# Some products and one copy move from VectorE to GpSimd, and the convolution history from GpSimd to ScalarE, in a streaming encoder layer

## The chip, the cores and the metric

The kernel runs on one core of a Trainium2 chip. A core has five engines with a queue of their own each, and each runs its queue in order: TensorE (PE, matrix products into PSUM; its weight loads are shown as PEld), VectorE (DVE), ScalarE (ACT), GpSimd (POOL) and SyncE (SP), which here only issues transfers (DMAs). An instruction that waits for a semaphore holds everything behind it in its queue. The metric is the time of one execution on the device in microseconds (us). The kernel before takes 2788.09 us, the median of three runs from 2786.51 to 2789.14.

## The reference, cut to what matters

One layer is applied to 1024 new positions (prompt) and 64 positions of a running stream (sample), together 1088 columns:

```
h    = RMSNorm(x) * (1 + scale1) + shift1
proj = h @ W_in                      # q, k, v, x, B, C, two gates, small columns, merge gates
q,k,v,x,B,C = silu(causal conv of width 4)   # the last 3 rows before the conv are an output, too
# mixer A, 8 heads, chunk by chunk (state s of 128 x 128):
lhs = I + strictly lower (k k^T * decay * beta)      # solved against v and k
u   = inv(lhs) (beta v) - inv(lhs) (beta exp(gam) k) s
o   = exp(gam) q s + (q k^T * decay) u
s   = exp(last) s + (k exp(last - gam))^T u
o   = rms(o) * gdn_norm * silu(z)
# mixer B, 8 groups of 4 heads, chunk by chunk (4 states of 128 x 64):
y   = (C B^T * decay * dt) x + exp(gam) C s ;   s = exp(last) s + B^T (wj x)
# then the merge of A and B, W_out, a norm, W_up, conv of width 3, silu gate, W_down, a norm
```

Here gam is the running sum of the log decays within a chunk and last its last value. The kernel's chunks are 128 positions: eight of the prompt and one of the sample.

## The kernel before

Channels lie on the 128 partitions and positions along the free dimension. A projection is done by tiles of 128 output channels; one tile takes three segments of 364, 364 and 360 columns, each of 24 matmuls into one of three PSUM buffers `pj` (8 slices of the model dimension, three matmuls each, because both factors are split in a rounded part and its rest: `whi`, `wlo` for weights). `load_w` brings a tile's weights (two DMAs into `wraw`), ScalarE makes `whi` by a cast (L114) and VectorE `wlo` by a subtraction (L115), one tile ahead of its use.

The first half of the kernel (the mixers, to about 1480 us) lays the chains of the mixers into the projections. Each chain is a generator; `weave` keeps a clock of PE work in `now` and takes the next piece of a chain when the latency named in the table `LAT` has gone by, else another 24 matmuls of a projection. The order of PE is written by hand that way, and fixed. The order on the other engines comes from the scheduler of the tile framework, which knows the dependences and its own estimates.

Three chains matter here, for head h of mixer A and group g of mixer B:

- `gdn_inverse`. `masked_decay` brings the decays `NU`: a DMA, a causal select on POOL (L587) and nine exponentials on ACT (L590). PE makes k k^T by chunks and DVE multiplies it in (L613). The diagonal is taken out by a product with the identity and a reduction (L618, L619), a reciprocal root of it follows in a dozen small DVE instructions on tile `kn` (L535 to L541), and `NU` is scaled (L626). Four DMAs (`dU`, L632) and three (`Ub`, L636) re-lay it, and the 32 x 32 blocks are inverted by 31 pairs of a DVE product and a reduction (L644, L647: the X loop). The result `Xb` is transposed in a copy (L649, XT below) and sent to memory and back by DMAs and transposed by DVE (L660). PE's products with it come `LAT["solve"]`, 74 us on `weave`'s clock, after the last k k^T.
- `gdn_scan`. The decays of q: a DMA, a select on POOL into `E` (L587), nine exponentials (L590), one more on ACT (L699), and two products with q (L700, L701). Then nine chunks in a row, of which each goes PE, DVE `r` (L740), PE, ACT `u` (L746), PE, DVE `st` (L756). At the end `o_norm` squares q and o on ACT (L777), adds the squares (L778), takes a reciprocal root of the column sums through a DMA, and scales `v` by it and by `gnorm` (L781).
- `ssd_mix`. For chunk c: a DMA of the decays into `gi`, a select on POOL (L821), four exponentials on ACT (L824), a fifth of `gi` (L826), and the decayed C (L827, half of C times the exponential, for four heads). `inputs` makes the matrices of the chunk one chunk ahead. In the chunk, the state is scaled (L874) and the new part added (L876).

`conv_steps` copies a projection's PSUM into `buf` by ACT and, at the last segment, copies the last three columns of prompt and sample into `ncm` by POOL (L517, L518).

Of the kernel before, what the change touches and what calls it, by code (L numbers as in the profile page):

```python
# [5 lines left out]

# [10 lines left out]
ALU = mybir.AluOpType  # L17
# [30 lines left out]
def body(tc, I, O):  # L48
# [28 lines left out]
    b_eps4 = bias_tile(4 * EPS, "beps4")  # L77

# [242 lines left out]
    with ExitStack() as c1:  # L321
# [183 lines left out]
        def conv_steps(w, ti, d):  # L505
            buf = tl(cv, [P, 1096], "buf", bufs=2)
            pool.memset(buf[:, 0:3], 0.0)
            pool.memset(d[:, CW:TW], 0.0)
            pool.tensor_copy(buf[:, 1027:1030], hist[:, ti, :])

            def evac(si, s, e, ps):
                if si < 2:
                    act.copy(buf[:, 3 + s:3 + e], ps[:, :e - s])
                else:
                    act.copy(buf[:, 3 + s:3 + TP], ps[:, :TP - s])
                    act.copy(buf[:, 1030:1094], ps[:, TP - s:T - s])
                    pool.tensor_copy(ncm[:, ti, 0:3], buf[:, 1024:1027])  # L517
                    pool.tensor_copy(ncm[:, ti, 3:6], buf[:, 1091:1094])  # L518
                    e = CW
                u = d[:, s:e]  # L520
                act.activation(u, buf[:, s:e], AF.Identity, bias=bcv[:, ti:ti + 1], scale=wcv[:, ti, 0:1])
                for i in range(1, 4):
                    dve.scalar_tensor_tensor(out=u, in0=buf[:, s + i:e + i], scalar=wcv[:, ti, i:i + 1], in1=u,
                                             op0=ALU.mult, op1=ALU.add)
                act.activation(buf[:, s:e], u, AF.Tanh, scale=0.5)
                dve.scalar_tensor_tensor(out=u, in0=buf[:, s:e], scalar=1.0, in1=u, op0=ALU.add, op1=ALU.mult)
            yield from project_steps(w, hx, evac)
# [70 lines left out]
        def gdn_inverse(h):  # L598
# [8 lines left out]
            for c0 in range(0, NC, 4):  # L607
                n = min(4, NC - c0)
                ps = tl(pp, [P, 4, P], "n")
                for c in range(c0, c0 + n):  # L610
# [7 lines left out]
            dve.tensor_tensor(out=dg, in0=NU[:, 0:8, :], in1=ident.unsqueeze(1).to_broadcast([P, 8, P]), op=ALU.mult)  # L618
# [7 lines left out]
            dve.scalar_tensor_tensor(out=NU, in0=NU, scalar=-1.0, in1=H.br.unsqueeze(2).to_broadcast([P, NC, P]),  # L626
                                     op0=ALU.mult, op1=ALU.mult)
# [21 lines left out]
            dve.tensor_copy(XT, X.rearrange("p j c -> p c j"))  # L649
# [41 lines left out]
        def gdn_scan(h):  # L691
# [8 lines left out]
            dve.tensor_tensor(out=gi[:, 0:8, :], in0=gi[:, 0:8, :], in1=chunks(q[:, 0:TP]), op=ALU.mult)  # L700
            dve.tensor_tensor(out=gi[:, 8, :], in0=gi[:, 8, :], in1=chunk(q, 8), op=ALU.mult)  # L701
# [70 lines left out]
        def o_norm(h):  # L772
# [5 lines left out]
            dve.tensor_tensor(out=sq[:, 0:CW + 1], in0=sq[:, 0:CW + 1], in1=q[:, 0:CW + 1], op=ALU.add)  # L778
            yield LAT["on"]
            yield from rsqrt_row(sq, (128 * EPS) ** 2 * 4)  # L780
            dve.scalar_tensor_tensor(out=v[:, 0:CW], in0=v[:, 0:CW], scalar=gnorm, in1=sq[:, 0:CW],  # L781
                                     op0=ALU.mult, op1=ALU.mult)
# [28 lines left out]
        def ssd_mix(g):  # L811
# [5 lines left out]
            def decay(c):  # L817
# [7 lines left out]
                if c > 0:  # L825
                    act.activation(gi, gi, AF.Exp, scale=-1.0)  # L826
                    dve.scalar_tensor_tensor(out=gi, in0=chunk(cm, c).unsqueeze(1).to_broadcast([P, 4, P]),  # L827
                                             scalar=0.5, in1=gi, op0=ALU.mult, op1=ALU.mult)
# [25 lines left out]
            for c in range(NC):  # L854
# [18 lines left out]
                if s is not None:  # L873
                    dve.tensor_tensor(out=sn, in0=s, in1=ebl[:, c, h4].unsqueeze(2).to_broadcast([P, 4, 64]),  # L874
                                      op=ALU.mult)
                    dve.tensor_tensor(out=sn, in0=pst, in1=sn, op=ALU.add)  # L876
                else:
                    dve.tensor_copy(sn, pst)
# [457 lines left out]
```

## Time and profile before

| | us |
|---|---|
| median of three runs | 2788.09 |
| the profiled execution | 2791.15 |
| its span in the trace | 2789.4 |
| PE busy in the span | 2726.9 (98%) |
| DVE busy | 1815.0 (65%) |
| ACT busy | 1257.5 (45%) |
| POOL busy | 185.5 (7%) |

The span runs from the first instruction to the end of the last; 1.8 us of the profiled execution lie around it. Busy time is the time in which an engine has an instruction in work. "Idle before" is the time in which it had none, and the releaser is what ended it. A chain of waits runs back from the last instruction through what released each.

### The profile page before, as it was taken

The numbers are of one execution on the slowest core, as the hardware profiler recorded it, in microseconds if no ns is written. First come the engines' busy times: TensorE is split into PE (matmuls) and PEld (weight loads), VectorE is DVE, ScalarE is ACT, GpSimd is POOL, SyncE is SP. The second block draws the span as 40 slices with busy tenths as digits, with TensorE's granted clock in tenths as the row PEclk, the third lists the DMA queues.
The fourth block names the chain that finished last, engine by engine and source line by source line (L and its number), as shares of the span: only waits on it lengthen the run. The fifth ranks groups of instructions, "written<-read, shape, count | busy, mean of one in ns | idle before, by whom it ended". The sixth has DMA issues, their size and how long they took to land.

```text
span 2789.4 us, 48767 instructions
## 1 busy us (share of the span) xinstructions
PE 2726.9 (98%) x18650; PEld 2638.5 (95%) x18650; DVE 1815.0 (65%) x3912; ACT 1257.5 (45%) x2888; POOL 185.5 (7%) x565
## 2 busy tenths in 40 slices
PE   6999999999999999999999999999999999999998
PEld 5999999999999999999999998999899999999998
DVE  5776579697887878777544557543766464555556
ACT  5644455465555545555443434212534242424244
POOL 0110001010010101101000000000000000000000
PEclk8999999999999999999999999999999999999999
DMA  6222323223241323323235765343211111111122
GB/s 228 96 67 89 112 66 110 79 81 110 71 115 61 112 75 95 98 81 100 69 100 200 257 199 172 123 142 92 85 50 46 46 43 41 46 45 47 39 61 73
DMA packets 212716, 266.72 MB, mean 96 GB/s; under 512 B 51995, under 2 KB 145019, under 8 KB 212483
## 3 DMA queue, kind: packets, MB, share of 16 engines
q1 hardware_dynamic: 212482, 263.62, 30.2%
q8 instruction: 146, 2.39, 0.4%
q14 instruction: 88, 0.71, 0.1%
HBM read 217.38 MB, written 46.13 MB: 94 GB/s over the span
## 4 chain that ended last, share of the span: by engine, by line
PE 88%; DVE 5%; DMA 4%; ACT 1%; issue 1%; SPq 0%; POOL 0%; DVEq 0%; ACTq 0%; POOLq 0%
PE pj L226 36%; PE pj L147 16%; PE sy L147 6%; PE gk L147 5%; PE gs L147 5%; PE sa L147 5%; PE sy L226 3%; PE gk L226 2%; DMA wada<-in_wada 2%; PE n L226 2%; PE gs L226 1%; DVE prod L644 1%; DMA gi<-gdr 1%; PE pj L1221 1%; DVE Xb L647 1%
## 5 line engine op out<-in xcount | busy, mean ns | idle before, releaser
L226 PE MATMUL pj<-h,whi 128*128 128x364 f32 x4560 | 1151.4, 334 | 1.6 <-DVE fz L897 1.6
L226 PEld LDWEIGHTS pj<-h,whi 128*128 128x128 f32 x4560 | 791.9, 188 | 8.6 <-issue 4.8
L226 PE MATMUL pj<-h,wlo 128*128 128x364 f32 x2280 | 747.5, 328 | 0.0
L147 PE MATMUL pj<-op,whi 128*128 128x364 f32 (+1 forms) x1904 | 476.6, 330 | 0.8 <-ACT op L188 0.6
L226 PEld LDWEIGHTS pj<-h,wlo 128*128 128x128 f32 x2280 | 428.7, 188 | 0.0
L114 ACT CAST whi<-wraw 128x512 fp32r<-128x512 f32 (+1 forms) x382 | 231.1, 617 | 370.3 <-PE pj L147 130.7
L147 PEld LDWEIGHTS pj<-op,whi 128*128 128x128 f32 x1904 | 337.2, 188 | 6.7 <-ACT op L188 1.6
L115 DVE TENSOR_TENSOR wlo<-wraw,whi 128x512 fp32r<-128x512 f32 (+1 forms) x382 | 258.0, 684 | 111.8 <-ACT whi L114 111.2
L147 PE MATMUL pj<-op,wlo 128*128 128x364 f32 (+1 forms) x952 | 312.5, 329 | 0.0
L1128 DVE SCALAR_TENSOR_TENSOR acc<-buf,wfc,acc 128x364 f32<-128x364 f32 (+1 forms) x264 | 156.6, 597 | 97.3 <-ACT acc L1126 93.2
L147 PEld LDWEIGHTS pj<-op,wlo 128*128 128x128 f32 x952 | 178.8, 188 | 0.0
L147 PE MATMUL sy<-op,whi 128*128 128x364 f32 (+1 forms) x672 | 167.8, 330 | 0.0
L147 PE MATMUL gs<-op,whi 128*128 128x364 f32 (+1 forms) x652 | 164.0, 331 | 1.2 <-ACT q L1005 1.0
L147 PE MATMUL sa<-op,whi 128*128 128x364 f32 (+1 forms) x644 | 161.4, 330 | 0.0
L147 PE MATMUL gk<-op,whi 128*128 128x364 f32 (+1 forms) x640 | 160.3, 331 | 0.0
L824 ACT ACTIVATE E<-E,dt 128x128 f32<-128x128 f32 x288 | 94.6, 396 | 80.1 <-POOL E L821 80.0
L147 PEld LDWEIGHTS sy<-op,whi 128*128 128x128 f32 x672 | 119.0, 188 | 1.0 <-issue 0.4
L147 PEld LDWEIGHTS gs<-op,whi 128*128 128x128 f32 x652 | 115.5, 188 | 3.5 <-ACT q L1005 1.3
L147 PEld LDWEIGHTS sa<-op,whi 128*128 128x128 f32 x644 | 114.0, 188 | 1.2 <-issue 0.6
L147 PEld LDWEIGHTS gk<-op,whi 128*128 128x128 f32 x640 | 113.7, 189 | 1.4 <-issue 0.6
L147 PE MATMUL sy<-op,wlo 128*128 128x364 f32 (+1 forms) x336 | 110.3, 328 | 0.0
L147 PE MATMUL gs<-op,wlo 128*128 128x364 f32 (+1 forms) x326 | 107.7, 330 | 0.0
(414 smaller groups left out, 4364.7 us busy)
## 6 DMA issues: line engine op xcount, KB each, us to landing
wraw<-in_win SPq DMA_DIRECT2D x158, 256.0 KB
wraw<-in_wup SPq DMA_DIRECT2D x88, 256.0 KB
gi<-gdr SPq DMA_DIRECT2D x72, 256.0 KB
wada<-in_wada SPq DMA_DIRECT2D x32, 512.0 KB
op<-spz SPq DMA_DIRECT2D x24, 544.0 KB
wraw<-in_wdown SPq DMA_DIRECT2D x40, 256.0 KB
spz<-fz SPq DMA_DIRECT2D x48, 182.0 KB
gt<-spg SPq DMA_DIRECT2D x48, 182.0 KB
```

Source lines behind the costliest of these rows:

```text
L114: act.copy(hi, src)
L115: dve.tensor_tensor(out=lo, in0=src, in1=hi, op=ALU.subtract)
L147: pe.matmul(pss[si][:, :e - s], lhsT=a[:, k, :], rhs=xk[:, b, s:e], start=(k == 0 and n == 0), stop=(k == nk - 1 and n == 2))
L226: pe.matmul(out, lhsT=lhsT, rhs=rhs, start=start, stop=stop)
L644: dve.tensor_tensor(out=prv, in0=X[:, 0:i + 1, 0:n].rearrange("p j c -> p c j"), in1=U[:, 0:i + 1, i:i + 1].rearrange("p j o -> p o j").to ...
L647: dve.tensor_reduce(out=X[:, i, 0:n], in_=prv, axis=mybir.AxisListType.X, op=ALU.add)
L824: act.activation(E[:, a, :], E[:, a, :], AF.Exp, bias=dt8[:, c, 4 * g + a:4 * g + a + 1], scale=-1.0)
L1128: dve.scalar_tensor_tensor(out=acc[:, c0:c1], in0=buf[:, i + c0:i + c1], scalar=wfc[:, ti, i:i + 1], in1=acc[:, c0:c1], op0=ALU.mult, op1= ...
L1221: pe.matmul(pss[m - m0][:, :n], lhsT=wts[m][a][:, k, :], rhs=fs[k][:, b, s:e], start=(k == 0 and i == 0), stop=(k == 3 and i == 2))
```

## The change

The instructions of nine lines of the mixers go from DVE to POOL: the product with the identity (L618), the scaling of `NU` (L626), the transposing copy XT (L649), the two products of q (L700, L701), the sum of squares (L778), the scaling of o (L781), the decayed C (L827) and the scaled state (L874). POOL gets plain products of two tensors only. So a factor that stood in the DVE instruction goes elsewhere: the minus sign into a small DVE product on nine columns, `gnorm` into an ACT instruction over `v`, the half of the decayed C into the bias of the exponential (log 0.5). The two copies into `ncm` become one ACT copy. Nothing else is changed; line numbers after L75 are two higher in the changed kernel.

```diff
+    b_half = bias_tile(math.log(0.5), "bhalf")
...
-                    pool.tensor_copy(ncm[:, ti, 0:3], buf[:, 1024:1027])
-                    pool.tensor_copy(ncm[:, ti, 3:6], buf[:, 1091:1094])
+                    act.copy(ncm[:, ti, :].rearrange("p (b c) -> p b c", c=3),
+                             buf[:, 960:1094].rearrange("p (b c) -> p b c", c=67)[:, :, 64:67])
...
-            dve.tensor_tensor(out=dg, in0=NU[:, 0:8, :], in1=ident.unsqueeze(1).to_broadcast([P, 8, P]), op=ALU.mult)
+            pool.tensor_tensor(out=dg, in0=NU[:, 0:8, :], in1=ident.unsqueeze(1).to_broadcast([P, 8, P]), op=ALU.mult)
...
-            dve.scalar_tensor_tensor(out=NU, in0=NU, scalar=-1.0, in1=H.br.unsqueeze(2).to_broadcast([P, NC, P]),
-                                     op0=ALU.mult, op1=ALU.mult)
+            dve.scalar_tensor_tensor(out=t, in0=t, scalar=-1.0, in1=beta[:, :, h], op0=ALU.mult, op1=ALU.mult)
+            pool.tensor_tensor(out=NU, in0=NU, in1=t.unsqueeze(2).to_broadcast([P, NC, P]), op=ALU.mult)
...
-            dve.tensor_copy(XT, X.rearrange("p j c -> p c j"))
+            pool.tensor_copy(XT, X.rearrange("p j c -> p c j"))
...
-            dve.tensor_tensor(out=gi[:, 0:8, :], in0=gi[:, 0:8, :], in1=chunks(q[:, 0:TP]), op=ALU.mult)
-            dve.tensor_tensor(out=gi[:, 8, :], in0=gi[:, 8, :], in1=chunk(q, 8), op=ALU.mult)
+            pool.tensor_tensor(out=gi[:, 0:8, :], in0=gi[:, 0:8, :], in1=chunks(q[:, 0:TP]), op=ALU.mult)
+            pool.tensor_tensor(out=gi[:, 8, :], in0=gi[:, 8, :], in1=chunk(q, 8), op=ALU.mult)
...
-            dve.tensor_tensor(out=sq[:, 0:CW + 1], in0=sq[:, 0:CW + 1], in1=q[:, 0:CW + 1], op=ALU.add)
+            pool.tensor_tensor(out=sq[:, 0:CW + 1], in0=sq[:, 0:CW + 1], in1=q[:, 0:CW + 1], op=ALU.add)
+            act.activation(v[:, 0:CW], v[:, 0:CW], AF.Identity, scale=gnorm)
...
-            dve.scalar_tensor_tensor(out=v[:, 0:CW], in0=v[:, 0:CW], scalar=gnorm, in1=sq[:, 0:CW],
-                                     op0=ALU.mult, op1=ALU.mult)
+            pool.tensor_tensor(out=v[:, 0:CW], in0=v[:, 0:CW], in1=sq[:, 0:CW], op=ALU.mult)
...
-                    act.activation(gi, gi, AF.Exp, scale=-1.0)
-                    dve.scalar_tensor_tensor(out=gi, in0=chunk(cm, c).unsqueeze(1).to_broadcast([P, 4, P]),
-                                             scalar=0.5, in1=gi, op0=ALU.mult, op1=ALU.mult)
+                    act.activation(gi, gi, AF.Exp, bias=b_half, scale=-1.0)
+                    pool.tensor_tensor(out=gi, in0=chunk(cm, c).unsqueeze(1).to_broadcast([P, 4, P]), in1=gi,
+                                       op=ALU.mult)
...
-                    dve.tensor_tensor(out=sn, in0=s, in1=ebl[:, c, h4].unsqueeze(2).to_broadcast([P, 4, 64]),
-                                      op=ALU.mult)
+                    pool.tensor_tensor(out=sn, in0=s, in1=ebl[:, c, h4].unsqueeze(2).to_broadcast([P, 4, 64]),
+                                       op=ALU.mult)
```

PE's instructions stand in the same order in both kernels. On the others the scheduler made new orders. The first place is POOL at the end of the scan of head 2, where the inverse of head 3 is still in its X loop; before:

```order
L508 MEMSET x_858_5922 128x65
L587 AFFINE_SELECT NU_6373<-NU_6373 128x1152
L587 AFFINE_SELECT E_5407<-gi_5406 128x1152
L508 MEMSET q_6348 128x65
L656 MEMSET prod_4832 32x9x32
L517 COPY ncm_592<-buf_5578 128x3
```

and in the changed kernel, at the same place:

```order
L510 MEMSET x_859_5910 128x65
L651 COPY prod_4817<-Xb_4722 108x352
L589 AFFINE_SELECT NU_6358<-NU_6358 128x1152
L780 TENSOR_TENSOR sq_5587<-sq_5587,q_1574 128x1092
L510 MEMSET q_6333 128x65
L589 AFFINE_SELECT E_5396<-gi_5395 128x1152
L658 MEMSET prod_4823 32x9x32
L702 TENSOR_TENSOR gi_5395<-gi_5395,q_4395 128x1024
```

The copy XT (L651 now) stands ahead of both selects, and the sum of squares (L780) between them. The inverse's X loop has to end before the copy can run.

The second place is ACT at the same point: the exponentials that wait for these selects, and what is behind them. Before:

```order
L777 ACTIVATE sq_5598<-v_4093 128x1092
L895 ACTIVATE fz_5437<-pj_5385 128x364
L590 ACTIVATE NU_6373<-NU_6373,ngam_595 128x128 x8
L590 ACTIVATE E_5407<-E_5407,ngam_595 128x128 x9
L699 ACTIVATE gi_5406<-gi_5406 128x1152
L895 ACTIVATE fz_5466<-pj_5441 128x360
L114 CAST whi_5470<-wraw_5472 128x512
```

and in the changed kernel:

```order
L779 ACTIVATE sq_5587<-v_4085 128x1092
L897 ACTIVATE fz_5426<-pj_5374 128x364
L781 ACTIVATE v_4085<-v_4085,gnorm_588 128x1091
L592 ACTIVATE NU_6358<-NU_6358,ngam_597 128x128 x4
L592 ACTIVATE E_5396<-E_5396,ngam_597 128x128 x9
L701 ACTIVATE gi_5395<-gi_5395 128x1152
L897 ACTIVATE fz_5455<-pj_5430 128x360
L116 CAST whi_5459<-wraw_5461 128x512
```

The `gnorm` instruction is new, and four exponentials of `NU` instead of eight stand ahead of those of `E`; the cast of the next weights is still behind all of `E`'s.

The third place is DVE in the inverse, where the second and third piece of k k^T are multiplied in, in the stretch about 421 us of the trace before. Before:

```order
L613 TENSOR_TENSOR NU_4430<-n_4622,NU_4430 128x512
L756 SCALAR_TENSOR_TENSOR st_4629<-st_4527,ebl_598,gk_4628 128x128
L523 SCALAR_TENSOR_TENSOR q_4405<-buf_4406,wcv_566,q_4405 128x364
L618 TENSOR_TENSOR Ub_4699<-NU_4430,ident_106 128x1024
L526 SCALAR_TENSOR_TENSOR q_4405<-buf_4406,q_4405 128x364
L613 TENSOR_TENSOR NU_4430<-n_4648,NU_4430 128x128
L619 TENSOR_REDUCE kn_4698<-Ub_4699 128x8
L827 SCALAR_TENSOR_TENSOR gi_4578<-cm_3700,gi_4578 128x512
L740 SCALAR_TENSOR_TENSOR r_4696<-gs_4635,neg_601,vt_4639 128x128
```

and in the changed kernel:

```order
L615 TENSOR_TENSOR NU_4420<-n_4612,NU_4420 128x512
L758 SCALAR_TENSOR_TENSOR st_4619<-st_4517,ebl_600,gk_4618 128x128
L525 SCALAR_TENSOR_TENSOR q_4395<-buf_4396,wcv_568,q_4395 128x364
L615 TENSOR_TENSOR NU_4420<-n_4638,NU_4420 128x128
L528 SCALAR_TENSOR_TENSOR q_4395<-buf_4396,q_4395 128x364
L621 TENSOR_REDUCE kn_4688<-Ub_4689 128x8
L840 TENSOR_TENSOR E_4570<-sa_4644,E_4570 128x512
L623 TENSOR_TENSOR Ub_4692<-NU_4420,ident_108 128x128
L878 TENSOR_TENSOR st_4666<-sy_4656,st_4666 128x256
L742 SCALAR_TENSOR_TENSOR r_4686<-gs_4625,neg_603,vt_4629 128x128
```

The product with the identity and the decayed C are gone from DVE; the reduction (L621) now waits for POOL's product, and `r` (L742) stands behind it.

## Rows read from the trace of the kernel before

**Rows 1.** Windows: stage; length; busy PE, PEld, DVE, ACT, POOL; clock; DMA.
```profile
70.00:1480.00 1410.00, 1394.31 (x10178) 1337.37 (x10179) 1035.32 (x2408) 737.19 (x1866) 143.38 (x372) 1.00 0.30 90
1480.00:2789.00 1309.00, 1284.66 (x8026) 1259.46 (x8020) 738.60 (x1435) 482.95 (x966) 39.64 (x176) 1.00 0.30 95
```

**Rows 2.** Waits of PE, 70 to 1480 us: total, times, longest.
```profile
PE gs L226 <- DVE r L740: 6.4, 10, 1.2
PE gk L226 <- ACT r L746: 3.0, 3, 2.0
PE n L226 <- issue: 2.5, 2, 1.5
PE pj L226 <- DVE fz L897: 1.6, 2, 1.2
PE gs L226 <- ACT vt L725: 1.3, 2, 1.0
```

**Rows 3.** Groups by line and form, DVE: busy us, mean ns | idle before.
```profile
L827 DVE SCALAR_TENSOR_TENSOR gi<-cm,gi 128x512 f32<-128x512 f32 x64 | 44.3, 692 | 23.1 <-ACT gi L826 21.8
...
L874 DVE TENSOR_TENSOR st<-st,ebl 128x256 f32<-128x256 f32 x56 | 23.5, 420 | 0.0
...
L778 DVE TENSOR_TENSOR sq<-sq,q 128x1092 f32<-128x1092 f32 x8 | 10.9, 1359 | 1.3 <-ACT sq L777 1.3
...
L700 DVE TENSOR_TENSOR gi<-gi,q 128x1024 f32<-128x1024 f32 x8 | 9.8, 1225 | 17.7 <-ACT gi L699 17.7
...
L649 DVE COPY prod<-Xb 108x352 f32<-108x352 f32 x8 | 6.5, 818 | 0.2
```

**Rows 4.** Groups by line and form, POOL, whole span.
```profile
L821 POOL TENSOR_SCALAR_AFFINE_SELECT E<-gi 128x512 f32<-128x512 f32 x72 | 54.6, 758 | 412.2 <-DMA gi<-gdr 233.8 <-PE sy L226 75.3 <-PE pj L226 19.3
L517 POOL COPY ncm<-buf 128x3 f32<-128x3 f32 x56 | 23.0, 410 | 429.2 <-ACT buf L515 429.2
```

**Rows 5.** Groups by line and form, ACT, whole span.
```profile
L516 ACT COPY buf<-pj 128x64 f32<-128x64 f32 x55 | 12.0, 218 | 0.0
...
L777 ACT ACTIVATE sq<-v 128x1092 f32<-128x1092 f32 x8 | 9.0, 1119 | 0.3
```

**Rows 6.** Timeline, POOL and DVE, head 3's boundary: start, length, instruction.
```profile
639.18 1.21 POOL L587 TENSOR_SCALAR_AFFINE_SELECT NU<-NU 128x1152 f32<-128x1152 f32 x1 [4.61 <-DMA NU<-gdr]
639.22 1.76 DVE L644 TENSOR_TENSOR prod<-Xb,Ub 108x300 f32<-108x300 f32 x1
...
641.51 0.77 DVE L644 TENSOR_TENSOR prod<-Xb,Ub 108x310 f32<-108x310 f32 x1
641.84 2.71 POOL L587 TENSOR_SCALAR_AFFINE_SELECT E<-gi 128x1152 f32<-128x1152 f32 x1 [1.45 <-DMA gi<-gdr]
```

**Rows 7.** Timeline, all engines, head 2's boundary, 479 to 494 us.
```profile
479.69 1.21 POOL L587 TENSOR_SCALAR_AFFINE_SELECT NU<-NU 128x1152 f32<-128x1152 f32 x1 [5.50 <-DMA NU<-gdr]
...
483.81 2.74 ACT L590 ACTIVATE E<-E,ngam 128x128 f32<-128x128 f32 x9 [0.43 <-POOL E L587]
...
485.04 0.81 DVE L649 COPY prod<-Xb 108x352 f32<-108x352 f32 x1
...
487.86 1.13 ACT L114 CAST whi<-wraw 128x512 fp32r<-128x512 f32 x2
...
490.47 0.69 DVE L115 TENSOR_TENSOR wlo<-wraw,whi 128x512 fp32r<-128x512 f32 x1
...
493.80 0.49 PE L226 MATMUL pj<-h,whi 128*128 128x364 f32 x2
```

**Rows 8.** Timeline, DVE and PE, end of head 4's solve.
```profile
821.58 0.47 DVE L660 STREAM_TRANSPOSE prod<-NU 32x288 f32<-32x288 f32 x1 [0.36 <-DMA NU<-dXT]
...
827.02 0.76 PE L226 MATMUL n<-prod,NU 32*32 32x32 f32 x36
```

**Rows 9.** Chain of waits, 250 to 268 us: start, length, piece.
```profile
253.69 1.37 DVE NU L626
...
259.20 5.26 DMA gi<-gdr
...
264.58 0.64 POOL E L821
```

More of the change, by code (lines that the diff above doesn't have):

```diff
@@ L7 @@
+import math
 from contextlib import ExitStack
```

## The prediction

> **What bounds the kernel now.** I read the windows first. Between 70 and 1480 us, the stage in which every edit lies, PE is busy 1394.3 of 1410 us and DVE 1035.3 [rows 1]. So PE is the bound, its order is the same in both kernels, and what the change can give back in this stage is PE's idle time, 15.7 us, or 0.56% of the run. A VectorE that is freer shows in the time only as far as PE waited for it.
>
> The waits of PE say where those 15.7 us are [rows 2]. The reader is to see that they are many and small: 6.4 us for `r` of the scan in ten waits, 3.0 us for `u` on ACT in three, of which one of 2.0, 2.5 us of two for the solve, 1.6 for a gate's evacuation by DVE, 1.3 for `vt`. DVE itself ended 8.0 us of them (6.4 and 1.6).
>
> **What is taken from DVE.** The 64 decayed C cost 44.3 us, the 56 scaled states 23.5 and the first eight at the same 0.42 another 3.4, the sum of squares 10.9, and L781 and L626, which are as wide, about as much each; the two products of 1024 columns 9.8 each, XT 6.5 [rows 3]. Together 44.3 + 26.9 + 32.7 + 19.6 + 6.5 = 130 us, 12.6% of what DVE does in the stage. The new small product on nine columns costs DVE next to nothing, eight times.
>
> **What POOL pays.** The trace of before has no product of two tensors on POOL. The nearest rows are its selects, which read one tensor: 1.21 us for 1152 columns [rows 7] and 0.64 for 512 [rows 9], that is 0.89 ns a column and 0.18 us to begin. The lower end takes these: 0.64, 0.41 for 256 columns, 1.1 to 1.2 for the wide ones; 64 of each of the first two and eight times 6.5 us give 119 us. For the upper end I let the second input cost a second pass: 1.09 and 0.64 us, 2.0 to 2.2 for the wide ones, with XT at 0.5; 70 + 41 + 8 x 11.4 = 202 us. I take the upper one, since two inputs are to be fetched; the sum below is that of a POOL that is some 1.6 times as slow as DVE (1.09 against 0.69 us). The Trainium skill ("GPSIMD Engine Reference", "Performance versus the Vector engine") has 4497 ns for a float32 addition of 2048 columns on GpSimd, against 2293 on VectorE; by that, 2.2 ns a column, POOL would pay about 209 us as an estimate. No run here shows it yet, and the sum would not move.
>
> POOL is busy 143.4 us of the stage [rows 1] and loses the copies into `ncm`, 23.0 us of one of the two lines [rows 4]. So it has the room: some 300 of 1410 us. Its queue is in order, so room is not the question; what an urgent select stands behind is.
>
> **What ACT pays.** 56 copies of six columns, nearest to its 64-column copy of 0.218 us, and eight passes over `v`, nearest to the square of 1.12 us [rows 5]: 12.2 + 9.0 = 21 us on an engine that is busy 737 of 1410. Lower end nothing, upper end the 21 us, if each stood ahead of something PE waits for. The evacuations have freed PSUM before the copy, and at the pass over `v` the scan is over: I take 0. The exponential with a bias is as long as before.
>
> **POOL and DVE get in each other's way.** At 639.18 POOL's select starts, 0.04 us before a DVE product of two SBUF tensors. That product takes 1.76 us, where a wider one takes 0.77 two steps later. At 641.84 the select comes second, behind DVE, and takes 2.71 us in place of 1.21 [rows 6]. One waits for nearly all of the other. The Trainium skill ("SBUF — State Buffer", "Who interferes with whom") says so as a rule: a VectorE instruction with two SBUF inputs contends with a GpSimd instruction that reads SBUF, through an exclusive lock for the whole instruction. The trace agrees (1.76 against 0.77 us). It is a rule against this change, and the second rival below works it out. In the sum I let POOL's 202 us hold up DVE for a third, 67 us, since about half of DVE's work reads PSUM or one SBUF tensor and POOL sometimes comes second; the bounds are none and all. DVE is then relieved by 130 - 67 = 63 us, 6% of its load.
>
> **On PE's path, what goes.** `r` waits behind other DVE instructions; half of the 130 us goes net, and I take a third of the 8.0 us: -2.5 us, bounds 0 and -8. The 2.0 us wait for `u` has another root, seen in the chain of waits: the scaling of `NU` on DVE at 253.69 holds the four `dU` DMAs on SP, behind these stands the DMA of the next decays at 259.20, and the select comes at 264.58 [rows 9], then ACT. In the changed order two decayed C and the product with the identity are out of DVE's queue between k k^T and the scaling (0.69, 0.69, 1.2 us); POOL's own product and scaling give back about 0.8 and 0.9. So `dU` comes about 1 us sooner, and I take -1.5 us with the small waits of the same kind. Bounds: -3, and +3 if POOL's scaling is late in its queue.
>
> The solve itself has cover: in head 4, where it is tightest, the last transposition ends at 822.05 and PE starts at 827.02 [rows 8], 5 us. The three POOL steps in it (identity, scaling, XT) cost 0.8 + 0.9 - 0.3 and a hand-over each, under 3 us, and DVE's part is shorter. I take 0. If more than 5 us came together PE would wait for the excess.
>
> **What comes new: XT ahead of the selects.** This is the step that I fear most. At head 2's boundary POOL's select of `NU` now runs at 479.69, `E`'s exponentials start on ACT at 483.81, the casts of the next weights at 487.86, the second `wlo` ends at 491.16, and PE takes these weights at 493.80 [rows 7]: a slack of 2.6 us. In the new order XT stands ahead of both selects and the sum of squares between them. Before, XT starts at 485.04. I let the X loop end 1 us sooner, since DVE loses about four products there (2.2 us) and POOL holds it up for about 1. Then: XT 484.0 to 484.6, select to 485.9, sum of squares 2.1 to 488.0, memset, select to 489.3. `E`'s exponentials start 5.5 us later; ACT's queue behind them is unchanged, so the first cast ends at 494.0 and its `wlo` at 494.7, where PE would want them at 493.8 and 494.1. The other half of the weights is wanted twelve matmuls later and comes in time. So PE waits about 1 us, where before it didn't. Heads 1, 3 and 5 have the like (in head 1 it is a select of mixer B with `vt` behind it); in head 4 XT comes after the selects, in 6 and 7 the selects came late already. Four times 1.3: +5 us. Bounds: 0 if the X loop ends 3 us sooner, and 4 us each (16) if it ends no sooner and POOL's steps wait for DVE.
>
> **Sum.** -2.5 - 1.5 + 5 = +1 us. It is made on the profiled execution (2791.15 us, span 2789.4, 1.8 around it), which lies 3.1 us above the median of the runs; as a difference it goes to the median: 2788.09 + 1 = 2789 us. A measurement of this kernel can tell about 0.2%, 5.6 us, from no change, so I forecast no change, with a range of its own from 2783 to 2794.
>
> **Rival 1: faster.** The X loop, in which DVE had no pause, ends 3 us sooner, so XT is no obstacle, and PE's waits that DVE and its followers end mostly go: 0.8 of 6.4 + 3.0 + 1.6 + 1.3 = 12.3, 10 us: 2778. For it: DVE is 73% busy in the stage and `r` is ready within a microsecond in most of 64 cases. Against it: the ten waits for `r` are short, and the pieces of the X loop that stand ahead of `r` stay on DVE.
>
> **Rival 2: slower, by the lock.** POOL's products hold DVE up for all of their 202 us, so that DVE has 72 us more to stand, not 63 less, and in pieces of up to 2.2 us, longer than any that it had. From there PE's waits for DVE and for `u` double, +11 us, and the boundary waits stay at +5, with the gain gone: about 2788 + 11 = 2799, or more. Rows 6 speak for it; against it that `r`, the kk products and the state update read PSUM and one SBUF tensor.
>
> **Rival 3: slower, by the boundary.** XT isn't ready sooner, so the selects are 7 us late and PE waits 4 us in each of four heads: +16 - 4 = +12, 2800. It decides from an X loop that ends less than 1 us sooner. Against it: DVE's load there does shrink.
>
> **Chances.** Forecast 0.46; rival 1 0.27; rival 2 0.10; rival 3 0.17. A tail of the forecast falls outside 0.2% on either side, and the rivals reach in as far, so: faster than 2782.5 0.27, within 0.46, slower than 2793.7 0.27. Eight times in ten I expect 2778 to 2800 us, which takes in the middle of all three rivals.
>
> **What would show it.** Right: PE's idle time in the stage stays within 10 to 21 us; a new wait of PE of about 1 us at the start of the tile that follows the boundary of heads 2, 3 and 5; `E`'s exponentials there 4 to 6 us later than the end of the scan in the trace of before; POOL's product of 512 columns at about 1.1 us, more when DVE is ahead of it; DVE's two-input products longer beside them, its busy time in the stage down by 60 us or so, not 130. Wrong: waits of PE for the solve (the `n` buffer) that grow by more than a microsecond a head; PE's idle time under 8 us; DVE's X loop several microseconds shorter or longer; a wait of PE of more than 3 us at any boundary.

## The result, and the profile after

The changed kernel takes 2829.97 us, the median of four runs (2828.76 to 2833.6), against 2788.39 for the kernel before: a ratio of 1.0158, 95% interval 1.0146 to 1.0171. It is 41.6 us slower, where 2789 us and a range of 2778 to 2800 were predicted. The profiled execution took 2829.06 us, its span is 2827.3, 37.9 more than before.

First the windows of the changed kernel. 1521 us is where TensorE (PE) has done the same number of matmuls as the kernel before at 1480 [rows 1].

```profile
70.00:1521.00 1451.00, 1405.42 (x10177) 1341.00 (x10176) 988.42 (x2233) 756.10 (x1929) 337.63 (x445) 1.00 0.29 87
1521.00:2827.00 1306.00, 1283.45 (x8027) 1258.57 (x8026) 736.44 (x1434) 483.38 (x966) 42.45 (x177) 1.00 0.30 95
```

All of the loss lies in the stage that was changed: 1451 us for the work of 1410. PE's idle time went from 15.7 to 45.6 us (+29.9), its busy time by +11.1. The rest of the kernel is 3 us shorter: PE waits about 2 us less there, and 1.7 us are a stretch that only the profiled execution of before has, in which PE's granted clock was at the lower of its two levels (1.2 GHz):

```profile
1591.40:1594.80 3.40, 3.40 (x26) 2.50 (x24) 0.53 (x1) 1.13 (x4) 0.00 (x0) 0.51 0.79 249
```

VectorE (DVE) is busy 46.9 us less. That isn't the whole relief, since a DVE instruction here often begins before the last one's end (0.08 us before the end of the reduction at 430.83 below) and busy time counts the overlap once. Added up one by one, DVE's instructions in the stage are 70 us shorter. 132 us were taken from it (the prediction's 130 leave out L701's 2.3) and 1.4 are the new small product, so 61 us came back as longer instructions.

PE's waits in that window, to be held against [rows 2]:

```profile
PE gs L228 <- DVE r L742: 33.8, 29, 2.6
PE n L228 <- ACT Ub L670: 4.5, 2, 2.3
PE sy L228 <- DVE yc L884: 1.8, 2, 1.1
PE pj L228 <- DVE fz L899: 1.8, 2, 1.0
PE gs L228 <- ACT vt L727: 1.4, 4, 0.7
```

The waits for `r` grew from 6.4 us in 10 to 33.8 in 29; that is 27.4 of the 29.9 us. PE's wait for `u`, 3.0 before, is down to 0.3. The trace of before was taken in an execution of 2791 us, and on the chips of the experiments the same kernel takes 2784, so its 6.4 us may be more than usual.

The groups of the moved instructions on GpSimd (POOL), whole span (L651 is XT, L784 the scaling of o):

```profile
L829 POOL TENSOR_TENSOR gi<-cm,gi 128x512 f32<-128x512 f32 x64 | 84.9, 1326 | 201.4 <-ACT gi L828 126.0 <-DVE cm L528 72.7 <-DMA Ub<-dU 2.7
...
L784 POOL TENSOR_TENSOR v<-v,sq 128x1091 f32<-128x1091 f32 x8 | 21.4, 2679 | 47.3 <-DMA sq<-rsd 47.3
...
L651 POOL COPY prod<-Xb 108x352 f32<-108x352 f32 x8 | 7.8, 976 | 18.5 <-DVE Xb L649 18.5
```

With the seven others (38.0, 21.3, 20.4, 19.2, 18.1, 7.0 and 5.2) POOL pays 243 us.

ACT pays for one thing more than was foreseen. The exponential that now carries the half as its bias is longer by 0.09 us, 5.9 us in all; the first line is of before, the second of the changed kernel. The runs below agree: 0.71 us wherever the bias is there (x2, z3, y1), 0.62 where it isn't (y2, w4).

```profile
L826 ACT ACTIVATE gi<-gi 128x512 f32<-128x512 f32 x64 | 39.8, 622 | 0.0
```

```profile
L828 ACT ACTIVATE gi<-gi,bhalf 128x512 f32<-128x512 f32 x64 | 45.7, 714 | 0.0
```

What stands ahead of a late `r` is seen in DVE's and POOL's timeline. The first place is the start of head 3's solve:

```profile
425.59 0.68 DVE L615 TENSOR_TENSOR NU<-n,NU 128x512 f32<-128x512 f32 x1
...
426.66 1.52 POOL L829 TENSOR_TENSOR gi<-cm,gi 128x512 f32<-128x512 f32 x1 [2.01 <-ACT gi L828]
...
428.14 2.65 POOL L620 TENSOR_TENSOR Ub<-NU,ident 128x1024 f32<-128x1024 f32 x1
430.83 1.22 DVE L621 TENSOR_REDUCE kn<-Ub 128x8 f32<-128x1024 f32 x1 [2.25 <-POOL Ub L620]
431.97 0.68 DVE L840 TENSOR_TENSOR E<-sa,E 128x512 f32<-128x512 f32 x1
...
433.10 0.34 DVE L742 SCALAR_TENSOR_TENSOR r<-gs,neg,vt 128x128 f32<-128x128 f32 x1
...
433.49 0.49 PE L228 MATMUL gs<-r,NU 128*128 128x128 f32 x2 [1.35 <-DVE r L742]
```

The second block of k k^T is ready at 426.27, but POOL's queue has a decayed C ahead, which came late from ScalarE (ACT). So the identity product runs from 428.14 to 430.79, DVE's reduction stands 2.25 us for it, and behind the reduction stands `r`. Ten microseconds on:

```profile
440.65 2.27 POOL L629 TENSOR_TENSOR NU<-NU,kn 128x1152 f32<-128x1152 f32 x1 [1.58 <-DVE kn L628]
440.87 0.68 DVE L840 TENSOR_TENSOR E<-sa,E 128x512 f32<-128x512 f32 x1
441.47 2.48 DVE L525 SCALAR_TENSOR_TENSOR bm<-buf,wcv,bm 128x364 f32<-128x364 f32 x2
...
443.88 0.35 DVE L742 SCALAR_TENSOR_TENSOR r<-gs,neg,vt 128x128 f32<-128x128 f32 x1
```

Here it is what the text below calls the lock: a DVE product of two SBUF tensors is held up by a POOL product. While POOL scales `NU`, DVE's E, one of whose inputs is in PSUM, takes its usual 0.68 us, but two conv steps with both inputs in SBUF take 2.48 in place of 1.20; the first ends at 443.32, after POOL at 442.93. `r` is late again (PE waits 1.55 us).

A third kind, at 787 us: the scaling of `NU` ends late, the four `dU` DMAs wait for it on SyncE (SP), the next decays' DMA stands behind them, then select, ACT, E, and `r` behind E.

```profile
773.67 2.28 POOL L629 TENSOR_TENSOR NU<-NU,kn 128x1152 f32<-128x1152 f32 x1 [1.58 <-DVE kn L628]
775.98 1.83 SPq L634 DMA_DIRECT2D dU<-NU  x4
778.40 0.41 SPq L821 DMA_DIRECT2D gi<-gdr  x1
...
784.23 0.64 POOL L823 TENSOR_SCALAR_AFFINE_SELECT E<-gi 128x512 f32<-128x512 f32 x1 [7.54 <-DMA gi<-gdr]
...
786.26 0.69 DVE L840 TENSOR_TENSOR E<-sa,E 128x512 f32<-128x512 f32 x1 [6.78 <-ACT E L826]
...
787.60 0.49 PE L228 MATMUL gs<-r,NU 128*128 128x128 f32 x2 [2.65 <-DVE r L742]
```

This is the chain of [rows 9], one engine further on. Sorted by the largest delay among the dozen DVE instructions ahead of each late `r`, the 33.8 us are: 9.1 after a wait for POOL's identity product, 8.2 after a wait for ACT, 5.8 after a stretched product, and 10.5 where DVE has simply come late with its queue, nearly all in the X loop, in which it has no pause (of the 6.4 us of before, 5.0 are of this kind). This sorting is a reading of the trace; the runs test it.

### The profile page after: what moved, and what is told of

Read it like the earlier page. It is cut to its first block, busy times and chain, and to the rows that moved or that the text cites. A ratio compares the mean times of both kernels' runs of the same rounds, so it can differ in the third digit from the quotient of the medians.

```text
span 2827.3 us, 48691 instructions
## 1 busy us (share of the span) xinstructions
PE 2737.1 (97%) x18650; PEld 2641.3 (93%) x18650; DVE 1765.5 (62%) x3737; ACT 1276.3 (45%) x2952; POOL 381.8 (14%) x637
## 4 chain that ended last, share of the span: by engine, by line
PE 80%; DVE 7%; DMA 5%; ACT 3%; POOL 2%; issue 2%; SPq 1%; DVEq 0%; POOLq 0%; ACTq 0%
PE pj L228 31%; PE pj L149 16%; PE sy L149 6%; PE sa L149 6%; PE gs L149 6%; PE gk L149 6%; DMA gi<-gdr 2%; PE sy L228 2%; DMA wada<-in_wada 2%; DVE prod L646 1%; PE gk L228 1%; PE gs L228 1%; PE n L228 1%; DVE Xb L649 1%; PE pj L1223 1%
## 5 line engine op out<-in xcount | busy, mean ns | idle before, releaser
L117 DVE TENSOR_TENSOR wlo<-wraw,whi 128x512 fp32r<-128x512 f32 (+1 forms) x382 | 267.7, 709 | 118.9 <-ACT whi L116 118.4
L646 DVE TENSOR_TENSOR prod<-Xb,Ub 108x2 f32<-108x2 f32 (+30 forms) x248 | 113.4, 457 | 6.0 <-POOL Ub L639 1.7
L829 POOL TENSOR_TENSOR gi<-cm,gi 128x512 f32<-128x512 f32 x64 | 84.9, 1326 | 201.4 <-ACT gi L828 126.0
```

What stands on the lines that cost most here:

```text
L117: dve.tensor_tensor(out=lo, in0=src, in1=hi, op=ALU.subtract)
L646: dve.tensor_tensor(out=prv, in0=X[:, 0:i + 1, 0:n].rearrange("p j c -> p c j"), in1=U[:, 0:i + 1, i:i + 1].rearrange("p j o -> p o j").to ...
L829: pool.tensor_tensor(out=gi, in0=chunk(cm, c).unsqueeze(1).to_broadcast([P, 4, P]), in1=gi, op=ALU.mult)
```

## The experiments

Each run but the whole change is compared with the kernel before on the same chip, whose median there was 2784 us; three theories are held against each other. Hand-over: DVE stands for POOL's identity product, with `r` behind. Lock: POOL's products hold up DVE's products of two SBUF tensors. Order: the scheduler's new order on DVE puts E ahead of `r`. The ratios, with 95% intervals, and PE's wait for `r` in 70 to 1521 us:

| on POOL (unless said otherwise) | ratio | interval | wait for `r`, us |
|---|---|---|---|
| kernel before | 1 | | 6.4 |
| whole change | 1.0158 | 1.0146–1.0171 | 33.8 |
| the solve's three alone (x1) | 1.0030 | 1.0019–1.0042 | 9.5 |
| mixer B's two alone (x2) | 1.0041 | 1.0026–1.0056 | 17.0 |
| decayed C alone (z3) | 1.0041 | 1.0027–1.0055 | 13.2 |
| q, sum of squares, scaling of o alone (w3) | 1.0020 | 1.0011–1.0029 | 5.7 |
| history on ACT alone (y4) | 0.9989 | 0.9979–0.9998 | 2.3 |
| change without the solve's three (x3) | 1.0070 | 1.0053–1.0086 | 14.7 |
| change without identity product (y1) | 1.0085 | 1.0068–1.0102 | 17.9 |
| change without decayed C (y2) | 1.0050 | 1.0035–1.0065 | 9.8 |
| change without both (w4) | 1.0033 | 1.0022–1.0044 | 5.6 |
| change, identity product in two halves (w5) | 1.0152 | 1.0135–1.0169 | 35.9 |
| change, products in pieces (y3) | 1.0207 | 1.0191–1.0222 | 28.1 |
| five of the steps left out (z1) | 0.9985 | 0.9976–0.9995 | 2.8 |
| decayed C left out (z2) | 0.9991 | 0.9982–1.0000 | 3.1 |
| before, with unread products (x4) | 1.0229 | 1.0213–1.0244 | 12.5 |
| before, with unread memsets (w1) | 1.0007 | 0.9998–1.0016 | 4.3 |

**Parts alone.** x1 takes the hunks of L618, L626 and L649, x2 those of L827 and L874, z3 that of L827, w3 those of L700, L701, L778 and L781, y4 the copy of L517. For example z3:

```diff
-                    act.activation(gi, gi, AF.Exp, scale=-1.0)
-                    dve.scalar_tensor_tensor(out=gi, in0=chunk(cm, c).unsqueeze(1).to_broadcast([P, 4, P]),
-                                             scalar=0.5, in1=gi, op0=ALU.mult, op1=ALU.mult)
+                    act.activation(gi, gi, AF.Exp, bias=b_half, scale=-1.0)
+                    pool.tensor_tensor(out=gi, in0=chunk(cm, c).unsqueeze(1).to_broadcast([P, 4, P]), in1=gi,
+                                       op=ALU.mult)
```

> The kernel before with only the three products of the solve on POOL (identity product, scaling of NU, XT). The whole change cost 41.6 us. Hand-over theory: DVE stands in its queue until POOL's identity product is done (2.3 to 4.6 us of idle time at the reduction in each head), the next r of the scan stands behind, and PE waits; then most of the loss is here: +20 to +35 us. Lock theory: POOL's products, whatever they are, hold up DVE's products of two SBUF tensors for as long as they last; then the loss goes by POOL's time, 46 of 243 us: about +8 us. Order theory (the scheduler's new order on DVE puts the product E of mixer B ahead of r, whoever makes the products): under +5 us as far as the order stays that of before.

> The kernel before with only mixer B's two products on POOL (64 decayed C with the half in the exponential's bias, 56 scaled states); 123 of the 243 us that POOL got. Hand-over theory: nobody waits soon for these two, so +0 to +5 us, or a gain of a few us from a freer DVE. Lock theory: half of the loss, about +20 us. Order theory: waits of PE for r with E ahead of it in DVE's queue, 9 of them and about 11 us in the changed kernel: +8 to +14 us.

> The kernel before with only the decayed C on POOL, 85 us of it. Mixer B's two together cost +10.4 us for 123 us of POOL. Lock theory: +7 us, and DVE's products longer by some 30 us in all. Order theory: +8 to +12 us, the same as without the product at all. Hand-over theory: 0 to +3 us, nobody waits soon.

> The kernel before with only the products outside the solve and mixer B on POOL: the two of q, the sum of squares, the scaling of o (gnorm on ScalarE); 70 us of POOL in pieces of 2.4 to 2.7. Lock theory, by the measured 11.5 us for 85 us of decayed C: +9 us. Sum of the runs so far (whole change without the solve +18, mixer B +10.4, history -3.5): +11. Relief of DVE alone: -2 us.

> The kernel before with only the conv history on ScalarE, 56 copies more there and 112 fewer on POOL. All three theories: no POOL product, so no change: -2 to +3 us. If it is +5 us or more, ACT's additions are a part of the loss.

Every group of products costs something by itself: +8.0 us (x1), +10.4 (x2), +11.5 (z3), +6.3 (w3); the history gains 3.5. The scaled states cost nothing beside decayed C (x2 against z3). The hand-over theory missed x1: with the solve alone the reduction waits for POOL 1.0 us in all. w3's loss is not in PE's waits for `r` (5.7 us); where it lies stays open. The parts (x1, x2, w3, y4) sum to +0.8%, the whole is +1.58%: half of the loss arises where parts meet.

**Parts undone.** y1, for instance:

```diff
-            pool.tensor_tensor(out=dg, in0=NU[:, 0:8, :], in1=ident.unsqueeze(1).to_broadcast([P, 8, P]), op=ALU.mult)
+            dve.tensor_tensor(out=dg, in0=NU[:, 0:8, :], in1=ident.unsqueeze(1).to_broadcast([P, 8, P]), op=ALU.mult)
```

> The changed kernel with the solve's three products back on DVE, all else on POOL as in the change. Hand-over theory: the loss shrinks from 41.6 us to 5 to 15. Lock theory: 197 of 243 us of POOL's products remain: about +34 us. Order theory: about +11 to +20 us, waits for r behind E remain.

> The changed kernel with only the identity product back on DVE. Measured so far: whole change +41.6 us, without the solve's three +18, the solve's three alone +8. So the three cost 23 us beside the other products and 8 us without them. Hand-over theory, in the form that these runs leave: on POOL the identity product comes behind decayed C, DVE's reduction stands 20.4 us in all for it (1.0 us in the run with the solve alone), and r stands behind the reduction; then most of the 23 us goes with this one product: +20 to +28 us. Lock theory: 20 of 243 us of POOL's products fewer: about +38 us. Order theory: +35 to +41 us.

> The changed kernel with only the 64 decayed C back on DVE, 85 of POOL's 243 us. Hand-over theory: the identity product has no decayed C ahead of it in POOL's queue, DVE's idle time at the reduction falls from 20.4 to under 8 us, and the loss to +10 to +20 us. Lock theory: 158 us of POOL's products are left: about +27 us, whatever the idle time at the reduction. Order theory: E of mixer B still ahead of r: about +30 us.

> The changed kernel with the identity product and decayed C back on DVE; 138 of 243 us of POOL's products remain. Undoing one took 20 us off (identity product) or 30 us (decayed C). If the 20 us are the meeting of the two in POOL's queue, undoing both gives little more than undoing decayed C alone: +10 to +16 us. If each has its own price, the loss is gone: -5 to +4 us. Lock theory by POOL's time, 0.13 us for each us: +14 to +18 us.

Beside the rest of the change (w4, +0.33%) the identity product adds 0.17% (y2), decayed C 0.52% (y1), the two together 1.25%: 0.56%, some 15 us, is their meeting (8 to 23 us, if the errors of the four ratios are independent). Without decayed C the reduction's wait is 2.7 us, without the identity product there is none; with both 20.4 in eight:

```profile
DVE kn L621 <- POOL Ub L620: 20.4, 8, 4.6
```

The sorted waits for `r` say the same: the 9.1 us behind the identity product are gone from y1 and y2, and those behind ACT fall from 8.2 to 3.7 and 3.0, about 14 us together.

No theory foretold all of these runs. The lock, counted by POOL's time, was right for x1 and 10 to 16 us too high for x2, x3, y1 and y2. The hand-over was right for y1 and y2 and wrong for x1, x2, x3 and z3. The order was right for x2, x3 and z3 and wrong for x1, y1 and y2.

**Is it the product's place in POOL's queue?** w5 leaves all work on POOL and makes the first half of the identity product ahead of that decayed C.

```diff
...
+                if c0 < 8:
+                    pool.tensor_tensor(out=dg[:, c0:c0 + 4], in0=NU[:, c0:c0 + 4, :],
+                                       in1=ident.unsqueeze(1).to_broadcast([P, 4, P]), op=ALU.mult)
                 yield LAT["kk"]
...
```

> The changed kernel with the identity product in two halves of 512 columns, the first made on POOL as soon as the first block of k k^T is there, ahead of a select and a decayed C; the second stays behind that decayed C. POOL's work is the same and one instruction longer per head. Place-in-the-queue theory: DVE's idle time at the reduction falls from 20.4 us to 5 to 12, and the time by 5 to 15 us, to +29 to +39 of before. Lock theory (only POOL's time counts): +42 to +46 us.

A miss: 1.0152, 41.7 us, and the reduction still waits 18.9 us. Its timeline shows why the split did little:

```profile
756.83 0.68 DVE L615 TENSOR_TENSOR NU<-n,NU 128x512 f32<-128x512 f32 x1
758.53 1.28 POOL L832 TENSOR_TENSOR gi<-cm,gi 128x512 f32<-128x512 f32 x1 [2.01 <-ACT gi L831]
759.77 1.27 POOL L619 TENSOR_TENSOR Ub<-NU,ident 128x512 f32<-128x512 f32 x1
761.07 1.22 DVE L624 TENSOR_REDUCE kn<-Ub 128x8 f32<-128x1024 f32 x1 [2.80 <-POOL Ub L619]
```

The second half is ready at 757.51 and still stands behind a decayed C that itself waits for ACT; it comes 3.5 us after the block in place of 4.5, and in the new order a conv step that DVE did during the wait stands behind it now. That the meeting costs 15 us is shown; that the place in POOL's queue is its channel was not confirmed by this run and stays a reading of the timelines.

**The lock by itself.** In x4 POOL makes additional products into a tile that nobody reads; in w1 it writes constants there instead, at the same places and for as long. (An additional piece is left out while o_norm uses that tile. The two edits are shown in one; the comments in it are added here.)

```diff
+        def extra(n, a, b):
+            if any(H.norm and not H.norm.done for H in heads):
+                return
+            scr = tl(cv, [P, 1096], "sq")
+            pool.tensor_tensor(out=scr[:, 0:n], in0=a, in1=b, op=ALU.mult)      # x4
+            for m in {256: (1000,), 512: (1092, 512)}.get(n, (1092, 1092, 512)):  # w1 in its place
+                pool.memset(scr[:, 0:m], 1.0)
...
+                    extra(512, cm[:, 0:512], cm[:, 512:1024])
```

> The kernel before, in which POOL makes 139 more products of two SBUF tensors of 256 to 1092 columns into a tile that nobody reads, about 158 us in all at the durations of the changed kernel, at the places of the moved ones; DVE keeps its own. Hand-over theory: nobody waits for them, so 0 to +5 us. Lock theory: 158 of 243 us, and DVE is not relieved of anything: +27 us or more, and DVE's products of two SBUF tensors longer by most of 158 us. Order theory: 0 to +5 us, since DVE's order is that of before.

> The kernel before, in which POOL writes constants into the tile that nobody reads, at the places and for about as long (some 200 us) as the additional products that cost 63 us; nothing is read from SBUF for them. Lock theory: DVE isn't held up, its stretched products sum to under 30 us (95 us with the products, 16 in before), so 0 to +12 us. POOL-queue theory (selects stand behind longer POOL work): +40 us or more, as with the products.

+63 us against +2. The two windows of 70 to 1480 us (x4, then w1) have POOL equally full:

```profile
70.00:1480.00 1410.00, 1356.69 (x9753) 1293.08 (x9753) 1086.88 (x2352) 713.87 (x1803) 325.32 (x506) 0.99 0.28 85
```

```profile
70.00:1480.00 1410.00, 1395.07 (x10191) 1337.73 (x10190) 1033.93 (x2409) 739.44 (x1868) 300.27 (x568) 1.00 0.29 90
```

The reader is to compare POOL's busy time (325 and 300 us) with the matmuls done (9753 and 10191; before 10178 [rows 1]). The additional products take 189 us, the memsets 195. One DVE group, the conv steps of mixer B's x (before 596 ns), shows how: 796 ns beside products, 596 beside memsets.

```profile
L529 DVE SCALAR_TENSOR_TENSOR x<-buf,wcv,x 128x364 f32<-128x364 f32 x96 | 76.4, 796 | 20.4 <-ACT x L527 18.8
```

```profile
L530 DVE SCALAR_TENSOR_TENSOR x<-buf,wcv,x 128x364 f32<-128x364 f32 x96 | 57.2, 596 | 20.3 <-ACT x L528 18.5
```

Take the lower quartile of a DVE group as its own time: the DVE instructions of the mixers that are over 0.1 us longer exceed it by some 95 us in x4, 13 in w1, 16 in before and 75 in the changed kernel. So a POOL that is busy to that extent cost nothing here; a POOL that reads SBUF beside DVE's two-input products did. The Trainium skill ("SBUF — State Buffer", "Who interferes with whom") has both halves: such a DVE instruction contends with a GpSimd one that reads SBUF, and not with one that only writes it. The runs agree (796 and 596 ns). Two limits. First, x4's products read `cm`, `k` and `q` and so free them later, which the memsets don't, and they fill POOL's queue otherwise: no wait of PE or DVE in x4's mixers ends with a POOL instruction, but ACT waits 107 us for POOL's selects of mixer B (80 in before, 78 in w1) and twice, 15.9 us in all, for a history copy behind the additional products. Second, x4 loses its time in another place than the changed kernel. PE's idle time is 37.6 us more than before, of which only 6.1 are for `r`:

```profile
PE sa L226 <- DVE xw L855: 14.1, 6, 3.1
PE gs L226 <- DVE r L749: 12.5, 18, 1.2
PE gs L226 <- ACT vt L734: 9.8, 8, 1.8
PE pj L226 <- DVE fz L908: 6.9, 3, 4.3
```

PE's busy time is 20.5 us more for the same matmuls: its granted clock was at the lower level for 34 us (3.4 in before), in seven stretches that each begin in or right after one of PE's waits. So x4 gives a price of POOL's reads in a kernel whose DVE keeps all its work, not the way in which `r` came late.

**Shorter holds.** y3 cuts every product but XT into pieces of 128 to 156 columns.

```diff
+                    for a in range(4):
+                        pool.tensor_tensor(out=gi[:, a, :], in0=chunk(cm, c), in1=gi[:, a, :], op=ALU.mult)
```

> The changed kernel, every product on POOL (XT left out) cut into pieces of 128 to 156 columns; the same work in 5 to 6 times as many instructions, POOL's time some 10 to 30% longer. If the length of a single hold is what counts (a DVE product stands 1.2 to 2.3 us behind one POOL product, with r behind it): DVE's stretched products fall to some 0.4 us over their own time and the loss falls to +20 to +32 us. If POOL's total time counts: +45 to +55 us. Hand-over theory: the identity product ends no sooner, so +40 us or more.

1.0207, +58 us. POOL's products take 365 us in the mixers in place of 233; DVE's stretches over 0.8 us fall from about 40 to one, all of its stretches from some 75 us to 34, and the time is worse all the same. The reduction waits 23.0 us and `r` costs PE 28.1; other waits grew, and PE's granted clock was at the lower level for 34 us (13.6 in the changed kernel). Cutting the products so doesn't help, then; what shorter holds would give at an equal POOL time isn't shown.

**What the relief is worth.** z2 leaves the decayed C's product out, z1 also those of L700, L701, L778 and L874 and all but two columns of L781; nothing takes their place.

```diff
-                    dve.scalar_tensor_tensor(out=gi, in0=chunk(cm, c).unsqueeze(1).to_broadcast([P, 4, P]),
-                                             scalar=0.5, in1=gi, op0=ALU.mult, op1=ALU.mult)
```

> The kernel before without five of the moved steps: the decayed C's product, the scaling of the state, the products of q, the sum of squares and the scaling of o are left out of the computation; nothing takes their place on POOL. DVE loses 112 us, POOL gets nothing: what the relief of DVE is worth by itself. The prediction's rival 1 had at most 10 us for all 130: -4 to -10 us. Lock theory: nothing locks, so the same. Order theory (the shorter queue lets the scheduler put E of mixer B ahead of r): +3 to +10 us, with waits for r of 10 us or more.

> The kernel before without the decayed C's product on any engine: the exponential goes to TensorE as it is, C and the half are left out. DVE loses 44 us, POOL gets nothing. Relief: -1 to -4 us. Lock theory: the same. Order theory: +6 to +10 us, most of what the two products of mixer B cost on POOL (+10.4).

A gain of 3.9 us for 105 us of DVE's instructions left out (by the times of before; the expectation has 112), 2.3 us for 44. For the decayed C the order theory falls. DVE's order in z2 is nearly that of z3 (at least 2227 of its 2343 instructions stand in the same order), and PE's waits for `r` are 13.2 us with the product on POOL (first line, z3), 3.1 without it (z2):

```profile
PE gs L228 <- DVE r L742: 13.2, 19, 1.6
```

```profile
PE gs L226 <- DVE r L740: 3.1, 7, 0.7
```

DVE's stretches sum to 42 us in z3 and 12 in z2. The product's being on POOL, where nobody waits for it soon, costs 13.8 us (z3 against z2), in which the longer exponential on ACT, 5.9 us of work, is contained. No run has the whole order of the changed kernel without its products on POOL, so for the whole change the order is not excluded.

**Versions.** w2 is y4 with the scaled states on POOL, z4 is y4 with the last stage's history on ACT as well.

```diff
-                    pool.tensor_copy(ncf[:, ti, 0:2], buf[:, 1024:1026])
-                    pool.tensor_copy(ncf[:, ti, 2:4], buf[:, 1090:1092])
+                    act.copy(ncf[:, ti, :].rearrange("p (b c) -> p b c", c=2),
+                             buf[:, 960:1092].rearrange("p (b c) -> p b c", c=66)[:, :, 64:66])
```

> The kernel before with the scaled states on POOL and the mixers' conv history on ScalarE; the parts of the change that cost nothing so far (decayed C and states together +10.4, decayed C alone +11.5, the history alone -3.5). By these: -3 to -5 us. Lock theory by POOL's time (38 us more, 41 us of small copies fewer): about 0.

> The kernel before with both conv histories (of the mixers and of the last stage) on ScalarE: 200 POOL copies of 2 or 3 columns become 100 ACT copies. The mixers' alone came out at 0.9989 of the time before, 3.5 us less. Lock theory: POOL's copies, 0.2 to 0.4 us each, hold DVE up as well, so -3 to -8 us. Otherwise the second half adds nothing: 0 to -3 us.

w2 is level with before (1.0000, 0.9991 to 1.0008), where a gain of 3 to 5 us was expected: with the history on ACT the scaled states on POOL cost about what the history gains. z4 at 0.9990 (0.9981 to 0.9999) is no better than y4. The one hunk that pays is the history on ACT: 2780.4 us against 2783.9, some 3.5 us faster, under the 0.2% that the prediction took for no change, but with an interval that leaves out 1. y4's stretches sum to some 14 us (before 16), so that gain isn't the lock's; PE's waits for `r` are 4.1 us less than in the trace of before, and the cause stays open.

## Why the prediction was wrong

- **The step that failed is "On PE's path, what goes: `r` waits ... I take a third of the 8.0 us: -2.5 us, bounds 0 and -8".** Measured: +27.4. It priced `r` by DVE's mean load, and its bounds excluded a loss. The load did fall, by 47 us of busy time, and load is worth little (z1: 3.9 us for 105). What counts is what stands directly ahead of `r` in DVE's queue: a reduction that waits for POOL, a conv step that the lock stretches, an E that waits for ACT. How much of the 27.4 each of them makes is read from the trace alone.
- **A wait that was seen and not priced.** The hand-over from the identity product to DVE's reduction, with `r` behind, went into the solve's slack as "a hand-over each". The reduction stood 20.4 us, 9.1 us of PE's waits follow it directly, and where identity product and decayed C meet some 15 us arise; that the hand-over is the channel of the 15 us stays a reading, since w5 didn't confirm it.
- **PE's busy time, no term:** +11.1. It was taken as fixed with PE's order; some 5 us of it are stretches at the lower clock (see the end), the other 6 stay open.
- **What POOL pays:** 202 us taken, 243 measured; 1.33 us for 512 columns (1.09 taken), 2.26 to 2.68 for the wide ones (2.0 to 2.2), XT 0.98 (0.5). POOL's durations include its own standing behind DVE: the shortest decayed C took 1.09 us, as taken, and those that began with 0.37 to 0.47 us of a conv step still to run took 1.52 to 1.61. At the shortest duration of each group POOL would pay 216 us. The estimate from the Trainium skill ("GPSIMD Engine Reference", "Performance versus the Vector engine"), 209 us, is near that sum and leaves such standing out.
- **The lock's share of DVE:** 67 us were taken, a third of 202; 61 were measured, a quarter of 243. DVE's relief, 70 us added up and 47 of busy time, is near the 63 predicted. That this share could cost more than all of the relief brings was the mistake: 85 us of POOL's products cost 13.8 us by themselves (z3 against z2), and x4's 189 us cost 63 where DVE keeps its work.
- **The SP chain, -1.5:** the wait for `u` went as predicted (3.0 to 0.3), but in heads 3 to 6 the scaling of `NU` ended 16.7 us after the second block of k k^T (15.6 to 15.8 before), later and not sooner, and the chain now ends in E with `r` behind: 5.3 us of the sorted waits come after such a wait of E for ACT. Its upper bound of +3 was too low.
- **The solve, 0:** nearly; waits for it 3.4 us before, 5.1 after.
- **The boundary, +5 (and rival 3):** didn't happen. In head 2 XT starts 2.8 us after the scan's last products start (9.3 before), since the scan had been held up more than the X loop; E's exponentials came 2.3 us later against the scan's end, not 5.5, and PE waited for no weights.
- **ACT, 21 us at no cost:** 18.9 more us, and the history alone is a gain. "The exponential with a bias is as long as before" was wrong: 0.71 us against 0.62. It is a link of each decayed C's chain; what it costs by itself no run shows.
- **Rival 2** had the mechanism and the sign, with a chance of 0.10. Its condition (all of POOL's time holds DVE) did not hold, and its price of 11 us was still a quarter of what came. Its sum is off, too: with the 5 us of the boundary that it keeps, 2788 + 11 + 5 is 2804, not 2799.

## What to carry to other kernels

Before moving work between engines, ask of the critical instruction what will stand ahead of it in its queue and what that waits for; a lower load on the engine is worth at most what the waits of the bound engine already show (here 3.9 us for 105 us of work, of 15.7 us of idle time). That nobody waits for the result of a two-input product on POOL doesn't make it free: it holds up DVE's two-input products, and here 85 us of it cost 13.8. POOL's time alone doesn't give the price, as x2, x3, y1 and y2 showed. Parts that are cheap alone should be timed together: two of them cost some 15 us by meeting.

## What the hardware showed beyond that

- GpSimd takes 2.0 to 2.6 ns a column for a product of two SBUF tensors in this kernel (1.33 us for 512 columns, 1.09 at the shortest; 2.26 us for 1152), and 0.43 to 0.58 us for a piece of 128 columns (y3). Memsets of 1092 columns (1.01 us, w1) leave VectorE's conv steps at 596 ns.
- An exponential of 512 columns on ScalarE took 0.71 us with the half as a bias and 0.62 without.
- VectorE's E, with one input in PSUM, keeps its 0.68 us beside GpSimd's products (0.683 on the mean in x4, too).
- After a wait PE can lose more than the wait. After the 1.87 us that ended at 953.4 us its granted clock was at the lower of its two levels (1.2 GHz) for 3.4 us:

```profile
953.90:957.30 3.40, 3.40 (x14) 3.40 (x13) 2.96 (x10) 2.75 (x7) 1.29 (x4) 0.50 0.14 39
```

  There are four such stretches in the mixers of the changed kernel and one in before; at 1.7 us each the three more are 5 of the 11 us by which PE's busy time grew.
